# Buffers given out by products since their release, and another order of column pairs in the seventh stage

## The chip, the cores and the metric

The kernel runs on one core of a Trainium2 chip. The metric is the device time of one execution in microseconds (us), the median of the runs shown. One execution is also profiled; its span and its rows are what the profile below shows.

## The reference, cut to what matters

One step of a small decoder over 1024 prompt positions and 8 single sampled positions, with a model width of 2048. One layer pools and gates (mixer A), one attends in windows of 128 (mixer B); both end in an output projection and a layer norm. All in float32.

```python
def pool_layer(x, ...):                       # mixer A
    z = x @ w_in                              # 2048 -> 4096: u and gate
    d, new_state = multiscale_pool(u, prefix, pos)
    d = einsum('btgc,gce->btge', d, w_grp) * scale
    y = (d * silu(gate)) @ w_out              # 2048 -> 2048
    return layer_norm(ALPHA * x + y, g_ln, b_ln), new_state
...
k, v = shared_kv(h, pos, w_kv)
...
def attn_layer(x, ...):                       # mixer B
    z = x @ w_in                              # 2048 -> 4096: q and gate
    o = attn_core(q, kb, vb, ...)             # window of 128, with sinks
    y = (o * silu(gate)) @ w_out              # 2048 -> 2048
    return layer_norm(ALPHA * x + y, g_ln, b_ln)
```

## The kernel before

**Stages.** The positions are cut into two chunks, 0 (512 positions) and 1 (512 and the 8 sampled ones, 520 columns). The stages follow each other as `PHASES` lists them: `ai` of chunk 0 and 1 (input projection of mixer A), `ao` of 0 and 1 (its output projection), `bi` of 0 and 1 (keys, values, queries and gates of mixer B), `bo` of 0 and 1. `bo` of chunk 0, written `bo0`, is the seventh stage, and `bo1` the eighth and last.

**Products.** Nearly all matrix work is done as pairs of output columns (two blocks of 128 rows at a time), each by Strassen's and Winograd's scheme with seven products (`seven`, `pair`; the first two pairs of a locked stage run side by side in `both`). A product is 24 matmuls (lines 703 to 705): eight blocks of the contraction, and for each of them high part by high part, high by low, and low by high, because each float32 operand is split into a part rounded to float32r and the rest. `self.i` counts the products done; `end()` runs after each, and hands out the work that is due then.

**Weights.** A product needs one weight block of 128x1024 (512 KB). `load_to` loads it on SP's queue (line 292) some products ahead of its use (`self.ahead` is 7, 4, 3 for load, cast, rest in most stages), ACT casts it to its high part (line 517), and DVE subtracts for its low part (line 534). Four of the seven blocks of a pair are sums of the input's quarters; chunk 0 of `ai` and `bi` adds them on DVE and stores them to DRAM through POOL's queue (`swia`, `swib`; `swoa` and `swob` are made ahead by `sum_gen`), and later stages load them back. In `bo0` six low parts (`LOW`: blocks 5 and 6 of the pairs 5, 6 and 7) are stored as well, at line 536 (tensors `low55` to `low76`), and the last stage loads them instead of subtracting again.

**The moving operand.** At the start of a stage the seven combinations of its input are loaded (line 847, 14 loads of about 520 KB), cast (857) and subtracted (866). Four of the seven were computed before (`t_ops`, lines 914 to 918: tensors `tx`, `tg`, `th`, `to`), stored through POOL and loaded from DRAM.

**What sets the order.** PE, DVE and ACT execute in the order of the source (`in_order`). The instructions of SP and POOL are placed by the recording layer's scheduler, which can move a DMA behind others when the buffer that it fills comes free later. Each queue is executed in order: a load at the head of SP's queue that waits for its buffer holds all loads behind it.

**Buffers.** One pool, `Mem`, serves everything above: 54 buffers (tags m0 to m53), most of 1040 float32 a partition, which are also given out in halves. `release` notes for each half when it was released; `full` and `half` choose by that note. In the kernel before, the note is a count of releases (`self.clock`), with 10 added for a buffer that a DMA to DRAM still reads (`free(True)`, or `stored`), and the buffer with the lowest note is given out. `half` prefers a buffer with one half free if that half was released more than five releases ago, or if no more than three whole buffers are left. A buffer given out is not a buffer that is ready: whoever writes it first waits for its last user by semaphore.

**The output stage.** `phase_out` walks the pairs 0 to 7 in order: `x_in(p)` loads the residual (line 1347) one pair ahead, `done` adds it (1363), and `shifted` subtracts a common shift, stores the pair to `p0` (1408), squares it and adds it to the sums of the layer norm; the last pair frees the shift's buffer. `build_stream` lists the weight blocks in the same order.

Of the kernel before, what the change touches and what calls it, by code (L numbers as in the profile page):

```python
# [61 lines left out]
ORDERL = (0, 5, 2, 1, 3, 4, 6)  # L62
ENGINES = (mybir.EngineType.PE, mybir.EngineType.DVE, mybir.EngineType.Activation)
NSLOT, NWIDE = 54, 52
KEEP0 = 1

SPLIT = 4, 5, 6, 7
# [4 lines left out]

LATE = ()
LOW = TAIL[-6:]
FORM = (0, 1)
X_KEEP = 5
X_AGE = 3
# [23 lines left out]
class Slot:  # L101
# [40 lines left out]
class Mem:  # L142


    def __init__(self, pool, n):
        self.pool = pool
        self.t = [None] * n
        self.f = [[0, 0] for _ in range(n)]
        self.clock = self.n = 0

    def new(self, i):
        self.n += 1
# [3 lines left out]
    def whole(self):  # L156
        return [i for i, (a, b) in enumerate(self.f) if a is not None and b is not None]

    def full(self, n=2 * TMAX):
        i = min((i for i in self.whole() if i < NWIDE or n <= 1024), key=lambda i: max(self.f[i]))  # L160
        self.f[i] = [None, None]
        self.new(i)
        return Slot(self, i, None, self.t[i][:])

    def half(self, n=TMAX):
        fits = lambda i: i < NWIDE or n <= 512
        part = [
            (a if b is None else b, i) for i, (a, b) in enumerate(self.f) if (a is None) != (b is None) and fits(i)
        ]
        if part and min(part)[0] > self.clock - 6 and len(self.whole()) > 3:  # L170
            part = []
        i = min(part)[1] if part else min((i for i in self.whole() if fits(i)), key=lambda i: max(self.f[i]))
# [12 lines left out]


class Entry:
# [7 lines left out]
class Kern:  # L195
# [188 lines left out]
    def build_stream(self):  # L384
        io = self.io
        w = []
        for kind, c, part in PHASES:
            seven, locked = (kind, c, part) not in PLAIN, (kind, c) in LOCKED
            pr = (lambda name, q: self.next_pairs(name, [q], False)) if seven else self.plain_pair
            if seven and c == 0:  # L390
                pr = lambda name, q: (lambda f: [f[i] for i in ORDER7])(self.first_pair(name, q))
            if kind == "ai":
                for n in range(*part):
                    g, gates = divmod(n, 2)
                    for q in (8 * gates + 2 * g, 8 * gates + 2 * g + 1):
                        if n:
                            w += pr("wia", q)
                        elif c == 0:
                            e = self.bare_pair("wia", q)
                            w += [e[0], e[2], e[1], e[3]] if q == 0 else e  # L400
                        else:
                            f = self.first_pair("wia", q, False)
                            w += [f[i] for i in ORDER7]
                    for h in range(2 if gates else 0):
                        w.append(self.lone(io["wg"][g][:, h * 1024 : (h + 1) * 1024]))
            elif kind == "bi":
                if part[0] == 0:
                    w += self.next_pairs("wkv", range(2), locked) if seven else pr("wkv", 0) + pr("wkv", 1)
                if seven:
                    for p in range(*part):  # L410
                        for q in (p, 8 + p):
                            if c == 1 and p in FORM:
                                f = self.first_pair("wib", q, False)
                                w += [f[i] for i in ORDER7]
                            else:
                                w += pr("wib", q)
                else:
                    for p in range(*part):
                        q, g = ((self.bare_pair if p in FORM else pr)("wib", q) for q in (p, 8 + p))
                        w += q[:2] + g[:2] + q[2:] + g[2:]  # L420
            else:
                name = "woa" if kind == "ao" else "wob"
                if (kind, c, part) != PHASES[-1]:
                    prs = [self.next_pair(name, q) for q in range(8)]
                    if (kind, c) == ("bo", 0):
                        for q in LATE:
                            prs[q] = self.first_pair(name, q)
                        for q, i in LOW:
                            prs[q][i].keep = self.low[q, i]
                    w += [pr[i] for i in ORDERL for pr in prs[:2]]  # L430
# [132 lines left out]
    def end(self):  # L563
# [765 lines left out]
    def phase_out(self, c, res, nxt, last=None):  # L1329
# [11 lines left out]
        pre, xs = [], {}  # L1341
        whole = 8 if last is None else SPLIT[0]
# [6 lines left out]
        x_in(0)  # L1349
        box0 = []  # L1350
        pairs = []
        for p in range(whole):
            if p < 2:
                self.at(8 + 4 * p, lambda p=p: x_in(p + 1))
            else:
                self.at(6, lambda p=p: x_in(p + 1))
            if p == 6 and nxt is not None:
                self.x_begin(nxt)
            box, z0, z1 = self.two(T)

            def done(p=p, box=box):
                s, x = box["s"], xs.pop(p)
# [2 lines left out]
                )  # L1365
                x.free()
                if c == 0 or last is not None:
                    self.shifted(c, p, s, pre, acc, p == whole - 1)
                    return
                nc.gpsimd.dma_start(self.act["p", c][:, 2 * p : 2 * p + 2, :], self.pair_view(s, T))  # L1370
                if p == 0:
# [7 lines left out]
                    s.free(True)  # L1379

            pairs.append((z0, z1, done))
            self.last = p == 7
            if p == 1:
                self.both(c, *pairs)
            elif p > 1:
                self.pair(c, *pairs[p])
        self.last = False
        if last is not None:
            self.phase_end(c, xs, x_in, pre, acc(), *last)
# [3 lines left out]
    def shifted(self, c, p, s, pre, acc, end):  # L1393
# [20 lines left out]
        def add():  # L1414
# [1121 lines left out]
```

## Time and profile before

| | |
|---|---|
| median of 3 runs | 2298.36 us (2297.86 to 2299.89) |
| the profiled execution | 2298.91 us, of which its span 2297.1 us |
| PE busy with matmuls | 2277.5 us (99%) |
| DVE busy | 1903.4 us (83%) |
| ACT busy | 1387.8 us (60%) |
| POOL busy | 220.0 us (10%) |
| moved by DMA | 660.36 MB, 287 GB/s in the mean |

The span runs from the first instruction's start to the last one's end. A matmul of 260 columns stands with 283 ns in the profile, but the next one starts after about 0.12 us: matmuls overlap, so PE counts as busy even where it is only just fed, and the time it lost is read from the waits. DVE and ACT do not overlap with themselves in that way, so their busy time says how full they are.

### The profile page before, as it was taken

To read this page: it belongs to the slowest core of one execution; us is meant where nothing else is said; L and a number is where in the kernel's file an instruction comes from. 1 tells how busy PE (TensorE), PEld (TensorE's weight loads), DVE (VectorE), ACT (ScalarE), POOL (GpSimd) and SP (SyncE) were. 2 spreads that over 40 slices of the span, in tenths; PEclk is the share of its full clock that TensorE was granted. 3 is DMA by queue.
4 is the path that set the end of the run, shared out by engine and by line. 5 is a ranking of instruction groups with operands and counts; after the bars stand their busy time and mean duration, and the time that the engine had idled before them with its cause. 6 is when DMAs were issued, how large, how long until landed. Compare 5 with 4: busy or idle time off the path is not lost.

```text
span 2297.1 us, 50586 instructions
## 1 busy us (share of the span) xinstructions
PE 2277.5 (99%) x20333; PEld 2207.7 (96%) x20333; DVE 1903.4 (83%) x2429; ACT 1387.8 (60%) x2552; POOL 220.0 (10%) x405
## 2 busy tenths in 40 slices
PE   9999999999999999999999999999999999999998
PEld 8999999999999999999879999999999999999998
DVE  8888789877878898998878888899876777788897
ACT  5554446544546446655466667695766668756666
POOL 0111110011010010000111111101110110000001
PEclk9999999999999999999999999999999999999999
DMA  7779679988889999999677666787787878799896
GB/s 259 272 258 310 234 250 328 322 302 290 308 301 318 349 347 370 327 380 368 205 272 244 237 230 224 267 285 266 252 272 231 267 254 294 242 335 361 293 348 227
DMA packets 258684, 660.36 MB, mean 287 GB/s; under 512 B 28016, under 2 KB 117136, under 8 KB 258448
## 3 DMA queue, kind: packets, MB, share of 16 engines
q1 hardware_dynamic: 214432, 499.64, 64.0%
q0 software_dynamic: 44016, 157.48, 17.8%
q8 instruction: 159, 2.61, 0.5%
q14 instruction: 77, 0.63, 0.1%
HBM read 476.64 MB, written 180.38 MB: 286 GB/s over the span
## 4 chain that ended last, share of the span: by engine, by line
PE 51%; issue 4%; DMA 3%; DVE 2%; ACT 1%; SPq 0%; POOL 0%; DVEq 0%; POOLq 0%; ACTq 0%
PE pD L703 13%; PE pD L705 13%; PE pD L704 13%; PE pO L2003 2%; PE pD L731 2%; PE pD L733 2%; PE pD L732 2%; PE pS L1925 2%; PE pS L1978 1%; DMA m<-swob 1%; DMA m<-in_woa 1%; PE pS L2003 0%; DMA m<-in_wob 0%; DMA m<-swoa 0%; DVE m L534 0%
## 5 line engine op out<-in xcount | busy, mean ns | idle before, releaser
L703 PE MATMUL pD<-m,m 128*128 128x260 f32 (+1 forms) x5088 | 1440.9, 283 | 5.2 <-ACT pD L642 2.9
L705 PE MATMUL pD<-m,m 128*128 128x260 f32 (+1 forms) x5088 | 1433.2, 282 | 4.1 <-DVE m L534 4.1
L704 PE MATMUL pD<-m,m 128*128 128x260 f32 (+1 forms) x5088 | 1433.6, 282 | 0.0
L703 PEld LDWEIGHTS pD<-m,m 128*128 128x128 f32 x5088 | 957.9, 188 | 14.8 <-issue 7.2
L705 PEld LDWEIGHTS pD<-m,m 128*128 128x128 f32 x5088 | 958.8, 188 | 5.9 <-DVE m L534 5.9
L704 PEld LDWEIGHTS pD<-m,m 128*128 128x128 f32 x5088 | 958.1, 188 | 0.5
L534 DVE TENSOR_TENSOR m<-m,m 128x1024 fp32r<-128x1024 f32 x684 | 825.3, 1217 | 84.5 <-ACT m L517 36.9
L517 ACT CAST m<-m 128x1024 fp32r<-128x1024 f32 x690 | 720.2, 1049 | 243.1 <-DVE m L356 100.3
L356 DVE TENSOR_TENSOR m<-m,m 128x1024 f32<-128x1024 f32 x128 | 156.4, 1222 | 13.4 <-DMA m<-in_wia 7.8
L866 DVE TENSOR_TENSOR m<-m,m 128x1024 fp32r<-128x1024 f32 (+1 forms) x118 | 143.9, 1224 | 3.9 <-ACT m L857 3.1
L857 ACT CAST m<-m 128x1024 fp32r<-128x1024 f32 (+1 forms) x118 | 123.4, 1054 | 4.0 <-DMA m<-in_x 2.4
L664 DVE TENSOR_TENSOR m<-pD,m 128x260 f32<-128x260 f32 (+1 forms) x92 | 39.0, 424 | 103.3 <-ACT pD L663 94.7
L676 ACT COPY m<-pD 128x260 f32<-128x260 f32 (+1 forms) x88 | 32.8, 372 | 119.5 <-PE pD L705 119.0
L1961 ACT ACTIVATE m<-m,sm 128x128 f32<-128x128 f32 x256 | 99.3, 391 | 0.0
L1203 PE MATMUL pD<-m,m 128*128 128x260 f32 (+1 forms) x528 | 91.5, 323 | 0.0
L651 ACT COPY m<-pD 128x260 f32<-128x260 f32 (+1 forms) x92 | 34.4, 374 | 92.7 <-PE pD L705 92.5
L731 PE MATMUL pD<-m,m 128*128 128x512 f32 x224 | 89.0, 398 | 0.0
L733 PE MATMUL pD<-m,m 128*128 128x512 f32 x224 | 88.3, 394 | 0.0
L732 PE MATMUL pD<-m,m 128*128 128x512 f32 x224 | 88.1, 393 | 0.0
L1203 PEld LDWEIGHTS pD<-m,m 128*128 128x128 f32 x528 | 79.4, 188 | 8.2
L648 ACT COPY m<-pD 128x260 f32<-128x260 f32 (+1 forms) x90 | 33.6, 373 | 88.8 <-PE pD L705 87.2
L642 ACT ACTIVATE pD<-pD 128x260 f32<-128x260 f32 (+1 forms) x90 | 33.2, 369 | 82.2 <-PE pD L705 81.5
(262 smaller groups left out, 2140.1 us busy)
## 6 DMA issues: line engine op xcount, KB each, us to landing
m<-in_wib SPq DMA_DIRECT2D x132, 512.0 KB
m<-in_wia SPq DMA_DIRECT2D x128, 512.0 KB
m<-swoa SPq DMA_DIRECT2D x64, 512.0 KB
m<-swob SPq DMA_DIRECT2D x64, 512.0 KB
swia<-m POOLq DMA_DIRECT2D x56, 512.0 KB, 4.7
m<-swia SPq DMA_DIRECT2D x56, 512.0 KB
m<-in_woa SPq DMA_DIRECT2D x48, 512.0 KB
swib<-m POOLq DMA_DIRECT2D x48, 512.0 KB, 4.1
```

The lines of the kernel that those rows point to most:

```text
L356: self.nc.vector.tensor_add(s[out].a[:, :1024], s[x].a[:, :1024], s[y].a[:, :1024])
L517: self.nc.scalar.copy(hi.r[:, :1024], self.stream[self.cast].src().a[:, :1024])
L534: self.nc.vector.tensor_sub(lo.r[:, :1024], s.src().a[:, :1024], hi.a[:, :1024])
L703: nc.tensor.matmul(ps[:, :TH], wh[:, s], h, start=new and k == 0, stop=False, skip_group_check=on)
L704: nc.tensor.matmul(ps[:, :TH], wh[:, s], l, start=False, stop=False, skip_group_check=on)
L705: nc.tensor.matmul(ps[:, :TH], wl[:, s], h, start=False, stop=k == 7, skip_group_check=on)
L731: nc.tensor.matmul(ps[:], wh[:, s], h, start=par == 0 and k == 0, stop=False)
L732: nc.tensor.matmul(ps[:], wh[:, s], l, start=False, stop=False)
L733: nc.tensor.matmul(ps[:], wl[:, s], h, start=False, stop=par == 1 and k == 7)
L857: self.nc.scalar.copy(h.r[:, :n], s.a[:, :n])
L866: self.nc.vector.tensor_sub(l.r[:, :n], s.a[:, :n], h.a[:, :n])
L1203: nc.tensor.matmul(ps[:, : cs.stop - cs.start], ws[:, s], d[:, cs], start=f0 and k == 0, stop=l0 and k == 3,)
```

## The change

`Mem` now notes for each half of a buffer the product in which it becomes ready (`tick + late`, where `tick` is `self.i` and `late` is 1 for a buffer that was read last and 5 for one that is being stored) and the count of releases. `wait` turns that into the products still to go, never under 0, and the count. `full` and `half` take the buffer with the fewest products to go, and among equal ones the one released longest ago. A free half is passed over for a whole buffer if it is not ready yet and more than three whole buffers are left. Nothing waits for the numbers 1 and 5: they only rank the buffers.

The seventh stage takes its pairs in the order 0, 1, 4, 5, 6, 7, 2, 3, in `build_stream` (weights), in `phase_out` (residual loads, products, stores). The shift's buffer is freed after the last pair of that order.

```diff
 NSLOT, NWIDE = 54, 52
+READ, STORED = 1, 5
...
+PAIRS = 0, 1, 4, 5, 6, 7, 2, 3
...
     def free(self, stored=False):
-        self.mem.release(self, 10 if stored or self.stored else 0)
+        self.mem.release(self, STORED if stored or self.stored else READ)
...
+    def wait(self, *fs):
+        return max(max(0, ready - self.tick) for ready, _ in fs), max(clock for _, clock in fs)
+
     def full(self, n=2 * TMAX):
-        i = min((i for i in self.whole() if i < NWIDE or n <= 1024), key=lambda i: max(self.f[i]))
+        i = min((i for i in self.whole() if i < NWIDE or n <= 1024), key=lambda i: self.wait(*self.f[i]))
...
-            (a if b is None else b, i) for i, (a, b) in enumerate(self.f) if (a is None) != (b is None) and fits(i)
+            (self.wait(a if b is None else b), i)
+            for i, (a, b) in enumerate(self.f) if (a is None) != (b is None) and fits(i)
         ]
-        if part and min(part)[0] > self.clock - 6 and len(self.whole()) > 3:
+        if part and min(part)[0][0] and len(self.whole()) > 3:
             part = []
...
-            self.f[s.i][h] = self.clock + late
+            self.f[s.i][h] = self.tick + late, self.clock
...
-                    prs = [self.next_pair(name, q) for q in range(8)]
+                    prs = {q: self.next_pair(name, q) for q in (PAIRS if kind == "bo" else range(8))}
...
         self.i += 1
+        self.mem.tick = self.i
...
-        for p in range(whole):
-            if p < 2:
-                self.at(8 + 4 * p, lambda p=p: x_in(p + 1))
-            else:
-                self.at(6, lambda p=p: x_in(p + 1))
+        order = PAIRS if self.ph == "bo0" else range(whole)
+        for n, p in enumerate(order):
+            m = order[n + 1] if n + 1 < whole else whole
+            self.at(8 + 4 * n if n < 2 else 6, lambda m=m: x_in(m))
...
-                    self.shifted(c, p, s, pre, acc, p == whole - 1)
+                    self.shifted(c, p, s, pre, acc, c == 0 and p == order[-1])
...
-            if p == 7:
+            if end:
                 self.l_sh[c].free()
```

In the built program PE's order is the same row by row, save for the buffers and for which pair's blocks `bo0` takes. DVE's and ACT's order differ in two short places each. SP's and POOL's order differ in many. In the rows that follow, `m52_468_4074` is buffer m52, the 468th tile that the pool gave out; the last number only names the instruction's tile. Line numbers of the changed kernel are 8 to 10 higher.

POOL's queue in the seventh stage, before: the stores of the four `to1` combinations for the last stage, of the finished pairs (`p0`) and of the six low parts, the last of which stands right before the last pair's store.

```order
L918 DMA to1_93<-m37_2742_25839 128x1040
L1408 DMA p0_89<-m50_2738_25807 128x1024
L918 DMA to1_93<-m5_2753_25945 128x1040
L536 DMA low55_103<-m52_2755_25955 128x1024
L536 DMA low56_104<-m48_2766_26055 128x1024
L1408 DMA p0_89<-m6_2764_26051 128x1024
L536 DMA low65_105<-m10_2781_26192 128x1024
L536 DMA low66_106<-m52_2795_26298 128x1024
L1408 DMA p0_89<-m37_2793_26294 128x1024
L536 DMA low75_107<-m51_2812_26439 128x1024
L536 DMA low76_108<-m0_2832_26557 128x1024
L1408 DMA p0_89<-m27_2830_26553 128x1024
```

The same queue in the changed kernel:

```order
L545 DMA low55_103<-m33_2691_25453 128x1024
L545 DMA low56_104<-m45_2704_25557 128x1024
L928 DMA to1_93<-m9_2710_25620 128x1040
L1417 DMA p0_89<-m18_2702_25553 128x1024
L545 DMA low65_105<-m3_2719_25698 128x1024
L928 DMA to1_93<-m15_2723_25732 128x1040
L545 DMA low66_106<-m30_2732_25806 128x1024
L928 DMA to1_93<-m26_2734_25835 128x1040
L1417 DMA p0_89<-m9_2730_25802 128x1024
L928 DMA to1_93<-m3_2745_25941 128x1040
L545 DMA low75_107<-m28_2747_25951 128x1024
L545 DMA low76_108<-m6_2758_26051 128x1024
```

All six low stores moved ahead by two pairs (fourteen products); behind the last of them now stand three stores of pairs (`p0`), where one stood.

SP's queue at the change from `ai0` to `ai1`, before: weights of both stages, and the moving operand (`in_x1`, `tx1`) of the next.

```order
L847 DMA m40_432_3801<-in_x1 128x4x260
L292 DMA m14_418_3660<-in_wia 128x1024
L292 DMA m26_429_3769<-in_wia 128x1024
L847 DMA m41_433_3803<-in_x1 128x4x260
L292 DMA m22_434_3807<-in_wia 128x1024
L847 DMA m38_440_3848<-tx1_90 128x4x260
L292 DMA m3_443_3854<-in_wia 128x1024
L847 DMA m23_439_3846<-tx1_90 128x4x260
L292 DMA m21_442_3852<-in_wia 128x1024
L292 DMA m30_450_3921<-in_wia 128x1024
L292 DMA m14_460_4031<-in_wia 128x1024
L292 DMA m20_468_4074<-in_wg 128x1024
```

The same twelve loads in the changed kernel:

```order
L300 DMA m53_434_3807<-in_wia 128x1024
L300 DMA m52_418_3660<-in_wia 128x1024
L300 DMA m42_429_3769<-in_wia 128x1024
L857 DMA m23_432_3801<-in_x1 128x4x260
L857 DMA m11_433_3803<-in_x1 128x4x260
L300 DMA m15_443_3854<-in_wia 128x1024
L300 DMA m51_450_3921<-in_wia 128x1024
L857 DMA m41_439_3846<-tx1_90 128x4x260
L857 DMA m45_440_3848<-tx1_90 128x4x260
L300 DMA m44_442_3852<-in_wia 128x1024
L300 DMA m52_468_4074<-in_wg 128x1024
L300 DMA m2_460_4031<-in_wia 128x1024
```

Each goes into another buffer; the block of tile 434 moved ahead of four loads, that of 450 ahead of three, and that of 460 fell behind the group weights of 468.

More of the change, by code (lines that the diff above doesn't have):

```diff
@@ L147, in __init__ @@
         self.t = [None] * n
-        self.f = [[0, 0] for _ in range(n)]
-        self.clock = self.n = 0
+        self.f = [[(0, 0), (0, 0)] for _ in range(n)]
+        self.clock = self.n = self.tick = 0
     def new(self, i):
@@ L167, in half @@
         part = [
-            (a if b is None else b, i) for i, (a, b) in enumerate(self.f) if (a is None) != (b is None) and fits(i)
+            (self.wait(a if b is None else b), i)
+            for i, (a, b) in enumerate(self.f) if (a is None) != (b is None) and fits(i)
         ]
-        if part and min(part)[0] > self.clock - 6 and len(self.whole()) > 3:
+        if part and min(part)[0][0] and len(self.whole()) > 3:
             part = []
-        i = min(part)[1] if part else min((i for i in self.whole() if fits(i)), key=lambda i: max(self.f[i]))
+        i = min(part)[1] if part else min(
+            (i for i in self.whole() if fits(i)), key=lambda i: self.wait(*self.f[i])
+        )
         h = 0 if self.f[i][0] is not None else 1
@@ L1351, in phase_out @@
         pairs = []
-        for p in range(whole):
-            if p < 2:
-                self.at(8 + 4 * p, lambda p=p: x_in(p + 1))
-            else:
-                self.at(6, lambda p=p: x_in(p + 1))
-            if p == 6 and nxt is not None:
+        order = PAIRS if self.ph == "bo0" else range(whole)
+        for n, p in enumerate(order):
+            m = order[n + 1] if n + 1 < whole else whole
+            self.at(8 + 4 * n if n < 2 else 6, lambda m=m: x_in(m))
+            if n == 6 and nxt is not None:
                 self.x_begin(nxt)
@@ L1381, in phase_out @@
             pairs.append((z0, z1, done))
-            self.last = p == 7
-            if p == 1:
+            self.last = n == 7
+            if n == 1:
                 self.both(c, *pairs)
-            elif p > 1:
-                self.pair(c, *pairs[p])
+            elif n > 1:
+                self.pair(c, *pairs[n])
         self.last = False
```

1 line of the change is left out of this document (added).

## The prediction

> **What bounds the kernel now.** I read the page first, then the waits of TensorE, then the busy time in stretches, and last the entry of the last stage in the timeline.
>
> The page's span and its row of TensorE's clock, then the waits of TensorE's matmuls in the run (releaser, us in total, times, longest; two of 0.2 us left out):
>
> ```profile
> span 2297.1 us, 50586 instructions
> PEclk9999999999999999999999999999999999999999
> ```
>
> ```profile
> PE pD L705 <- DVE m L534: 4.1, 9, 0.9
> PE pD L703 <- ACT pD L642: 2.9, 3, 1.3
> PE pD L703 <- ACT m L657: 1.7, 2, 1.1
> PE pD L749 <- DVE m L2253: 1.3, 1, 1.3
> PE pD L703 <- ACT m L2188: 0.6, 1, 0.6
> PE pD L1630 <- POOL area L1656: 0.6, 1, 0.6
> PE pO L974 <- DVE m L958: 0.3, 1, 0.3
> ```
>
> They sum to 11.5 us, 0.5% of the span, and the clock was full in every slice. So TensorE sets the time, its own work isn't touched by the change, and 11.5 us less what the start and the end need is all that a better feeding can bring. What a worse feeding can cost has no such lid.
>
> Where the waits lie, from the busy time in stretches (stretch, its length, PE, PEld, DVE, ACT, POOL busy with counts, clock, DMA share, GB/s):
>
> ```profile
> 0.00:100.00 100.00, 96.51 (x577) 85.88 (x578) 83.58 (x102) 58.11 (x77) 6.37 (x19) 1.00 0.73 255
> 300.00:400.00 100.00, 98.08 (x778) 95.48 (x777) 95.25 (x108) 57.02 (x80) 7.91 (x17) 1.00 0.88 299
> 900.00:1000.00 100.00, 98.82 (x817) 97.95 (x816) 93.16 (x104) 62.49 (x87) 4.28 (x8) 1.00 0.97 350
> 2080.00:2100.00 20.00, 20.00 (x172) 20.00 (x171) 13.75 (x15) 12.23 (x18) 1.55 (x4) 1.00 0.96 365
> 2100.00:2120.00 20.00, 20.00 (x171) 20.00 (x170) 19.91 (x20) 14.31 (x18) 1.20 (x3) 1.00 1.04 366
> 2120.00:2140.00 20.00, 18.23 (x149) 17.79 (x148) 20.00 (x21) 15.87 (x23) 0.53 (x1) 1.00 1.03 383
> ```
>
> TensorE is idle 3.49 us in the first 100 us, 1.92 at the entry of the second stage, 1.18 at that of the fourth, and 1.77 between 2120 and 2140, at the entry of the last. DVE is full in all of these (95.25 and 93.16 of 100, 20.00 of 20), and the DMA engines in the last (1.04, 1.03). Between the entries there is next to nothing.
>
> **The change part by part.**
>
> *Order of pairs.* No instruction is added or removed. What moves at the end of the seventh stage is six stores of low parts, on POOL's queue. Two matmuls on one line, three apart, give the pace, and the POOL rows of the timeline the places (start, length, idle before):
>
> ```profile
> 2039.73 0.28 PE L703 MATMUL pD<-m,m 128*128 128x256 f32 x1
> ...
> 2040.08 0.28 PE L703 MATMUL pD<-m,m 128*128 128x256 f32 x1
> ```
>
> ```profile
> 2062.11 0.53 POOL L536 DMA_DIRECT2D low<-m  x1 [0.60 <-DVE m L534]
> ...
> 2080.47 0.53 POOL L536 DMA_DIRECT2D low<-m  x1 [0.37 <-DVE m L534]
> 2086.56 0.53 POOL L536 DMA_DIRECT2D low<-m  x1 [5.55 <-DVE m L534]
> ...
> 2101.38 0.53 POOL L536 DMA_DIRECT2D low<-m  x1 [1.24 <-DVE m L534]
> 2110.51 0.53 POOL L536 DMA_DIRECT2D low<-m  x1 [8.60 <-DVE m L534]
> ```
>
> A product is 24 matmuls of 0.117 us (0.35 / 3), 2.8 us; two pairs are fourteen products, 39 us. So the stores at 2101.38 and 2110.51 go to about 2062 and 2071, and the first from 2062.11 to about 2023. The `p` stores keep their places, since each position still ends one pair.
>
> What stood in the way there, by the waits between 2090 and 2135, the ACT rows of the timeline, and the row of the chain that ended last:
>
> ```profile
> ACT m L517 <- DMA m<-swob: 4.1, 4, 2.7
> PE pD L703 <- ACT m L657: 1.1, 1, 1.1
> PE pD L703 <- ACT pD L642: 0.6, 1, 0.6
> ```
>
> ```profile
> 2129.07 1.06 ACT L517 CAST m<-m 128x1024 fp32r<-128x1024 f32 x1 [2.67 <-DMA m<-swob]
> ...
> 2130.98 0.37 ACT L657 COPY m<-pD 128x260 f32<-128x260 f32 x1
> ```
>
> ```profile
> 2117.81 11.18 DMA m<-swob
> ```
>
> A weight block took 11.18 us from its issue at 2117.81; ACT stood 2.67 us for it, the copy of line 657 is queued behind that cast, and TensorE waits 1.1 us for the copy. The 0.6 us ahead of it has the same form. All of it is DMA bandwidth: a stretch with a share of 1.03 moves 383 GB/s. A low store is 524,288 bytes, 1.4 us at (366 + 383) / 2 GB/s. Two of them out of this stretch make its later loads land 2.8 us sooner, which is more than the 2.67 us that ACT stood.
>
> The Trainium skill ("DMA: Bandwidth & Descriptors", section on the anatomy of one DMA) fits a transfer as about 2.0 us fixed and its bytes at 436 GB/s, by which the two would free 2.4 us, a little under 2.67; the trace's full stretches stay at 366 and 383, so I keep the larger figure.
>
> What is late next is DVE. Its first idle time after the crowd:
>
> ```profile
> 2143.21 0.43 DVE L664 TENSOR_TENSOR m<-pD,m 128x260 f32<-128x260 f32 x1 [1.30 <-PE pD L705]
> ```
>
> At 2143.21 it had waited 1.30 us for TensorE, so a TensorE that comes 1.77 us sooner finds DVE 0.47 us behind here. The term lies between 1.30 and 1.77 if the loads are what counts, and is 0 if DVE's queue inside the crowd, which has no idle time at all, is already what feeds TensorE. I take -1.5; ends -1.8 and 0.
>
> Where the stores go, the cost is that of two low stores in a stretch like 2080 to 2100: it holds two (at 2080.47 and 2086.56), with a share of 0.96, and TensorE lost 0.00 there. I take 0; ends 0 and +1.1 (the wait above, if it comes up there). The buffers of the low parts are also back 39 us sooner at the crowded end, which I count in the same term. Of the stores of pairs, 2 and 3 change places with 6 and 7: pairs 2 and 3 are now stored last, as 6 and 7 were, and are wanted only in the last stage's layer norm: 0.
>
> *The rule for buffers.* It changes which buffer a load or a cast gets, so whom it waits for, and with that SP's order. The waits of SP's queue (same columns), and the landing times of the low stores:
>
> ```profile
> SPq L292 <- PE pD L705: 342.7, 152, 8.9
> SPq L292 <- DVE m L534: 182.8, 88, 9.2
> SPq L292 <- DMA to<-m: 43.6, 9, 8.7
> SPq L292 <- DMA swoa<-m: 29.9, 7, 8.5
> ```
>
> ```profile
> DMA to landing us min/median/max: 5.4/7.7/8.6
> ```
>
> A load waits mostly for the last reader of its buffer, 2.3 us in the mean (342.7 / 152), and in a few cases 8.5 us for a store. Ten releases are, by the tile numbers in SP's order (34 tiles, 434 to 468, over five weight loads, about 7 a product), one and a half products, 4 us: shorter than a store's 5.4 to 8.6. Five products are 14 us, which covers it. So the waits for stores (73.5 us in the two rows) should fall, and loads will more often take a buffer that was only read. But nothing behind SP is idle for it in mid-stage: weights are issued seven products ahead and cast four ahead, which leaves three products, 8.5 us, and TensorE doesn't wait there. Only at the entries, where the pool is short and DVE full, does a load's time pass on. For the second stage's entry (waits from 340 to 420):
>
> ```profile
> PE pD L705 <- DVE m L534: 1.9, 3, 0.9
> PE pD L703 <- ACT pD L642: 1.3, 1, 1.3
> DVE m L356 <- DMA m<-in_wia: 1.3, 1, 1.3
> ```
>
> DVE lost 1.3 us there on one load, and is full else; SP's new order moves blocks both forward and back in the same place. Ends: -1.3 (that load comes in time) and +4.6 (two more waits of the mean length, in a crowd where nothing hides them). I take 0, since the moves go both ways. The few moved rows on DVE and ACT lie in stages where TensorE doesn't wait: 0.
>
> Sum: -1.5 + 0 + 0 + 0, from the profiled execution's 2298.91 to 2297.4. The median of the runs stands 0.55 below that execution: 2296.9.
>
> **The rivals.**
>
> *DVE hides it.* DVE's 19.91 and 20.00 of 20 speak for it: if its subtractions feed TensorE just in time, earlier loads change nothing, and the buffers' rule cancels out. Against it: the two waits there end on ACT rows behind a DMA, none on DVE's line 534. Time: unchanged, 2298.4.
>
> *The rule helps at every entry.* Of the 11.5 us, 3.5 are in the first 100 us, where the pool has hardly been round once, and 0.6 at the end (line 1630). If four fifths of the other 7.4 go, 5.9: 2292.5. For it: SP's waits for stores. Against it: at the second and fourth entries the longest part is DVE's own queue.
>
> *A load gets a buffer that is still read* (slower). A buffer read in the last product counts as ready in the next one, although its reader may stand far back on a full DVE (a wait for line 534 of up to 9.2 us is in the rows). Such a load at SP's head holds all behind it. In mid-stage the 8.5 us cover it; at an entry, where a load alone took 11.18 us, they don't, and each further us passes through ACT and DVE to TensorE. It decides as soon as two such heads fall into the entries of stages 2, 4 or 8: two mean waits are 4.6 us, with one long one among them 2.3 + 8.9 less the 1.5 won and some slack, about 6: 2304. For it: block 460 fell back in SP's order at the second entry. Against it: the old rule had the same blindness.
>
> The Trainium skill ("TensorE: Matmul & The Clock Gate", Part 1) has an idle stretch of about 3.4 us halve TensorE's clock for the next window; by that a wait of the long kind would cost some 1.7 us more. The longest wait here is 1.3 us and the clock row is full, so no run here shows it.
>
> **How the numbers follow.** Forecast (between 2295.5 and 2297.9): 0.43. DVE hides it (2298.4, give or take 1): 0.22. Every entry (2290.5 to 2293.8): 0.21. Slower (2303 and more): 0.14. A difference under 0.2%, 4.6 us, is what runs of this kernel can't tell from none: faster 0.23 (the third case and a little of the first), same 0.63, slower 0.14. The range from 2291.5 to 2303 leaves out the far part of the two outer cases, under 0.2.
>
> **What would show it.** The low stores of line 536 some 39 us earlier; in the crowd of the last entry ACT's wait for `swob` under 1 us, and TensorE busy over 19.5 of 20 where it was 18.23. SP's waits for `to`, `swoa` and `g` smaller, those for line 705 larger. The second and fourth entries within 1 us of before. I am wrong if the crowd keeps its 1.77 us with the stores gone (then DVE feeds it), or if new waits on line 534 or 642 stand at an entry.

## The result and the profile after

The changed kernel takes 2302.73 us, the median of 15 runs (2298.73 to 2308.2), beside 2298.86 us of before (15 runs, 2296.62 to 2301.21): a ratio of 1.0017, 95% interval 1.001 to 1.0024, slower by some 3.9 us. The forecast was 2296.9. The profiled execution took 2303.87 us, 1.1 above its median.

The page of the changed kernel, its span and clock row, and then the waits of TensorE's matmuls (line waiting, releaser, us in total, times, longest; eight smaller rows left out):

```profile
span 2302.1 us, 50582 instructions
...
PEclk9999999999999999999999999999999999999999
```

```profile
PE pD L715 <- DVE m L543: 4.9, 10, 0.9
PE pD L713 <- ACT pD L652: 2.3, 2, 1.3
PE pD L713 <- ACT pD L673: 2.2, 1, 2.2
PE pD L759 <- DVE m L2262: 1.3, 1, 1.3
PE pD L713 <- ACT m L667: 1.2, 1, 1.2
PE pD L713 <- ACT m L2197: 0.7, 1, 0.7
...
```

One wait is of a kind that before did not have: 2.2 us, once, for the copy of line 673. Stretches of the changed kernel (columns as in the prediction), and last the third one's counterpart in the kernel before:

```profile
900.00:1000.00 100.00, 99.35 (x824) 98.69 (x824) 93.62 (x101) 64.67 (x90) 4.27 (x8) 1.00 0.97 354
...
2120.00:2140.00 20.00, 20.00 (x167) 19.81 (x166) 20.00 (x20) 14.39 (x20) 0.53 (x1) 1.00 1.05 390
880.00:900.00 20.00, 17.77 (x148) 17.46 (x148) 15.45 (x18) 10.30 (x15) 1.27 (x2) 1.00 1.04 395
```

```profile
880.00:900.00 20.00, 20.00 (x172) 20.00 (x171) 17.64 (x20) 14.05 (x19) 1.27 (x2) 1.00 0.99 332
```

TensorE has the 20.00 of 20 at the last stage's entry that the order of pairs was to bring (also from 2127 to 2147, where the work of before's 2120 to 2140 now lies), and loses 2.23 between 880 and 900, at the entry of the fourth stage, where before lost nothing.

The two traces have the same 20333 matmuls in the same order, so the start of the k-th in one less that in the other says where time is lost. In us, at points of before's time, for the kernels that matter below:

```
                  340   880   900  1100  1260  1590  1660  1930  1970  2110  2150  2230  2270
changed kernel   -0.1  +0.2  +3.0  +1.7  +2.2  +2.5  +5.7  +5.7  +7.0  +7.1  +5.1  +4.9  +4.9
rule_only        -0.3  -0.5  +3.1  +1.5  +4.8  +5.1  +5.8  +5.9  +5.9  +5.6  +6.5  +6.4  +6.4
pairs_only       -0.0  -0.0  -0.0  -0.6  -0.6  -0.6  -0.6  -0.1  +1.5  +1.7  -0.2  +2.8  +2.8
pairs_p20        +0.1  -0.2  -0.2  +0.3  +0.3  +0.3  +0.3  +0.3  -0.0  +0.1  -1.8  -1.8  -1.9
wob9             -0.5  -1.0  -0.8  -1.8  -1.0  -1.2  +1.4  +1.5  +2.1  +2.1  +0.2  +0.1  +0.0
stored8          -0.3  -0.2  +6.8  +8.7  +9.7 +10.7 +10.7 +14.0 +16.6 +16.5 +14.6 +15.5 +15.5
to_loads6        -0.3  -0.7  -0.6  -1.3  -1.6  -1.7  +4.9  +6.7  +6.6  +6.6  +5.7  +5.6  +5.6
loads_shy1_ao    -1.0  -0.6  -0.4  -2.2  -1.4  -1.4  -1.3  -0.8  -1.4  -1.2  -2.4  -2.5  -2.5
```

The changed kernel loses 2.8 us at one place near 889, 3.2 between 1590 and 1660 in steps of at most 1.3, and 1.3 near 1950, and wins 1.3 between 900 and 1100 and 2.0 at 2124 to 2131. The rest is small.

Small entries of this table may be chance. Up to about 1960 `pairs_only` and `pairs_p20` are the program of before, instruction by instruction. Still the first loses 1.6 us between 1930 and 1970 and the second does not, and between 900 and 1100 they move by 0.6 and 0.5 us in opposite directions.

**The place near 889.** SP's waits in the changed kernel from 862 to 876, then rows of SP's, ACT's and TensorE's timelines (start, length, idle before):

```profile
SPq L857 <- DMA swob<-m: 6.9, 1, 6.9
SPq L300 <- DMA swob<-m: 3.0, 1, 3.0
```

```profile
865.52 0.38 SPq L1357 DMA_DIRECT2D m<-in_x  x1
872.89 1.48 SPq L857 DMA_DIRECT2D m<-g  x3
...
875.77 0.59 SPq L300 DMA_DIRECT2D m<-in_woa  x1
```

```profile
887.12 1.04 ACT L526 CAST m<-m 128x1024 fp32r<-128x1024 f32 x1 [5.18 <-DMA m<-in_woa]
888.07 1.05 ACT L867 CAST m<-m 128x1040 fp32r<-128x1040 f32 x1
889.03 0.36 ACT L673 COPY pD<-pD 128x256 f32<-128x256 f32 x1
```

```profile
889.45 0.39 PE L713 MATMUL pD<-m,m 128*128 128x256 f32 x1 [2.23 <-ACT pD L673]
```

A load of `g` has been given a buffer out of which a block of `swob` is still being stored. SP stands 6.9 us for the landing, between 865.52 and 872.89, and everything behind that load stands with it. The block of in_woa that ACT wants next goes out at 875.77, in a burst with the other loads that were held, and has landed only by 887.12, 11.3 us later; ACT stands 5.18 us for it, and the copy of line 673, which TensorE needs, is queued behind that cast on ACT. Before, SP's longest wait for a store in this stretch is 0.9 us, the same block goes out 5.6 us sooner, and the copy (line 663 there) starts 3.5 us sooner:

```profile
SPq L847 <- DMA p<-m: 0.9, 1, 0.9
```

```profile
870.15 0.81 SPq L292 DMA_DIRECT2D m<-in_woa  x1
```

```profile
885.56 0.37 ACT L663 COPY pD<-pD 128x256 f32<-128x256 f32 x1
```

**What the rule did to SP.** The view of SP's waits, changed kernel:

```profile
SPq L300 <- PE pD L715: 320.6, 144, 8.9
SPq L300 <- DVE m L543: 144.2, 76, 7.4
SPq L466 <- DMA swoa<-m: 94.1, 19, 9.0
...
SPq L300 <- DMA swoa<-m: 49.5, 10, 8.9
...
SPq L300 <- DMA to<-m: 20.1, 3, 9.9
```

All its rows add to 1683 us, before's to 1689: SP stands as long as ever, but for something else. The waits for stores (`rows` left out) went from 307 us in 77 to 407 in 97, those for `swoa` alone from 45 to 144 (before had 29.9 us on line 292 and this row):

```profile
SPq L457 <- DMA swoa<-m: 15.0, 4, 5.4
```

In the two programs one can count who takes a buffer that had been stored last. Of 354 such, loads on SP's queue took 116 before and 152 after, casts and subtractions most of the rest; in the products that run from about 350 to 910 us it was 22 of 73 and 50 of 76. Yet these buffers were on average older: 4.8 products since their release, 4.3 before.

Two lines of the code explain it, as I read them; the runs on who takes the stored buffers, further down, test it. Under the new rule a stored buffer comes of age on a product's edge, and `begin` calls `load_to` first, before `prep_to` and `cast_to`: a load is the first to see it. Under the old one a buffer's rank rises release by release, so it may come up anywhere in a product. A cast or a subtraction that takes such a buffer comes late in its own engine's queue and seldom waits: in before ACT and DVE together stood 8.3 us for stores, in eight waits, the longest 2.1. A load waits at the head of SP's queue.

### The profile page after: what moved, and what is told of

The parts are those of the page before. It is cut to its first block, busy times and chain, and to the rows that moved or that the text cites. A ratio compares the mean times of both kernels' runs of the same rounds, so it can differ in the third digit from the quotient of the medians.

```text
span 2302.1 us, 50582 instructions
## 1 busy us (share of the span) xinstructions
PE 2278.9 (99%) x20333; PEld 2207.5 (96%) x20333; DVE 1905.4 (83%) x2429; ACT 1386.4 (60%) x2552; POOL 220.0 (10%) x405
## 4 chain that ended last, share of the span: by engine, by line
PE 86%; DVE 6%; DMA 3%; issue 1%; ACT 1%; SPq 0%; DVEq 0%; POOL 0%; ACTq 0%; POOLq 0%
PE pD L713 24%; PE pD L715 23%; PE pD L714 23%; PE pD L1213 3%; PE pO L2012 2%; PE pD L741 2%; PE pD L743 2%; PE pD L742 2%; DVE m L543 2%; PE pS L1934 1%; PE pS L1987 1%; DVE m L364 1%; DVE m L876 1%; DMA m<-rows 0%; DMA m<-in_wia 0%
## 5 line engine op out<-in xcount | busy, mean ns | idle before, releaser
L686 ACT COPY m<-pD 128x260 f32<-128x260 f32 (+1 forms) x88 | 32.7, 372 | 113.7 <-PE pD L715 112.6
L1970 ACT ACTIVATE m<-m,sm 128x128 f32<-128x128 f32 x256 | 99.2, 390 | 0.0
L661 ACT COPY m<-pD 128x260 f32<-128x260 f32 (+1 forms) x92 | 34.4, 374 | 90.5 <-PE pD L715 90.5
L1983 ACT ACTIVATE m<-m,sm 128x128 f32<-128x128 f32 x256 | 81.9, 393 | 4.3 <-DVE sm L1978 4.1
```

## The experiments

Each was timed in five rounds beside the kernel before on the same chip; ratios are to before, with 95% intervals.

**The parts alone.** `pairs_only`: the kernel before with the new order and all that hangs on it, and the old rule.

```diff
+PAIRS = 0, 1, 4, 5, 6, 7, 2, 3
...
+        order = PAIRS if self.ph == "bo0" else range(whole)
```

> The kernel before with the order of pairs 0, 1, 4, 5, 6, 7, 2, 3 in the seventh stage, and the old rule for buffers. Theory A (the two parts act apart: the order wins what was forecast for it, the rule loses more): TensorE's waits of 1.77 us at the entry of the last stage go, nothing else moves, about 2 us under before: 2296 to 2298. Theory B (the order itself is the loss, for instance because pairs 2 and 3 are stored last): 2300 to 2303, as in the changed kernel.

2300.95 us, ratio 1.0007 (0.9998 to 1.0016): theory B's range, 3 us above theory A's, though 1 is still inside the interval. The 1.9 us at 2124 to 2131 came as theory A has it, and two losses stand beside it: 1.6 us between 1930 and 1970, which is chance of this execution, since the program is still that of before there, and 3.1 between 2200 and 2230. The second one in its rows (SP's waits 2180 to 2200, all engines' waits to 2217):

```profile
SPq L297 <- DMA p<-m: 9.6, 1, 9.6
```

```profile
DVE m L1463 <- DMA m<-h: 3.3, 1, 3.3
...
PE pD L711 <- DVE m L540: 2.6, 2, 1.5
```

The same form as near 889, under the old rule: a load of swob stands 9.6 us for a store to `p`, a load of `h` behind it reaches DVE 3.3 us late, and TensorE waits 2.6 us for DVE. Whether the order must cost this, or a buffer's chance does, is left to `pairs_p20`.

`rule_only`: the changed kernel with the old order.

```diff
-PAIRS = 0, 1, 4, 5, 6, 7, 2, 3
+PAIRS = 0, 1, 2, 3, 4, 5, 6, 7
```

> The changed kernel with the pairs in the order 0 to 7 again; the new rule for buffers stays. Theory A: the rule alone costs 6 to 7 us (2.4 at the entry of the fourth stage, some 2.7 between 1594 and 1651, 1 at the entry of the seventh stage), so 2304 to 2306, and TensorE waits 2.2 us near 889 as in the changed kernel. Theory B (the order is the loss): 2298 to 2300.

2305.48 us, ratio 1.0027 (1.0017 to 1.0037): theory A. The rule is the loss, and TensorE again waits near 889, 1.85 us.

**The two numbers of the rule.** `stored8` has eight products for a stored buffer, `stored4` four; `read2` has two for one that was read.

```diff
-READ, STORED = 1, 5
+READ, STORED = 1, 8
```

> The changed kernel with eight products for a stored buffer instead of five. Theory A1 (five products are too short for a store that stands in POOL's queue behind DVE; SP then waits for its landing and holds every load behind it): SP's waits for stores, 407 us in 97 in the changed kernel, fall under half, the wait near 889 goes, and the time falls by 3 to 6 us to 2297 to 2300. Theory A2 (the loss is read buffers handed out while still read): younger read buffers, 1.75 products old instead of 2.04, so SP's waits for readers grow and the time is the same or more, 2302 to 2307.

2314.93 us, ratio 1.0069 (1.0056 to 1.0081): both theories fail. SP's waits for stores fell only to 332 us, and the wait near 889 grew to 4.9 us. Waiting longer does not keep loads off stored buffers: they still took 128 of 353, and SP stood 7.1 us for swob between 860 and 896.

> The changed kernel with four products for a stored buffer instead of five. With eight the time rose by 12 us, because the buffers that were only read are then given out younger (1.75 products old in the mean instead of 2.04). If that balance is what counts, four give 2299 to 2301.5, with fewer waits for readers at the entries; if stores are what SP must be kept from, four give 2304 to 2308.

2305.89 us, ratio 1.0038 (1.0025 to 1.0052): the second reading, with 450 us of waits for stores and a wait of 3.2 us near 889. So of four, five and eight the five is best (six and seven were not run), and neither of the others mends the place.

> The changed kernel with two products for a buffer that was only read instead of one; a stored one keeps five. Stored buffers are then taken a little younger (4.5 products in the mean instead of 4.8). Theory A1 (stores): SP's waits for stores stay or grow, and the time stays at 2302 to 2305. Theory A2 (readers): SP's waits for readers fall and with them TensorE's waits; 2297 to 2300.

2301.13 us, ratio 1.0012 (1.0003 to 1.0021): between the two ranges. Against A1 the time fell 1.6 us below the changed kernel's; against A2 SP's waits for readers did not fall (1107 us in the changed kernel, 1115 here). SP stands 6.4 us for swob here too, but some 10 us later: the block of in_woa that came too late in the changed kernel had gone out at 869.83, ahead of that wait, and TensorE does not wait near 889. Where the wait stands decides, not its length.

**The rule by stages.** `old_mid` deals by the old rule in the second to fourth stages, `new_mid` in the other five.

```diff
+OLD = ("ai1", "ao0", "ao1")
...
+        if self.old:
+            return max(key for _, _, key in fs), 0
...
+        self.mem.old = getattr(self, "ph", "ai0") in OLD
```

> The changed kernel with the old rule for buffers in the second, third and fourth stages (about 350 to 1090 us) and the new one elsewhere; the new order of pairs stays. Theory C (the new rule's loss is SP standing for a store in these stages, above all 7 us near 870 for a store of swob, behind which the loads of the fourth stage's entry come late): SP's waits for stores between 350 and 910, 205 us in the changed kernel and 81 before, fall to about 80, the wait of 2.2 us near 889 goes, and the time falls by 2 to 3 us: 2299.5 to 2301. Theory D (any new deal of buffers puts some load of an entry behind a long wait, wherever the rule changes): the wait near 889 goes, but others of 1 to 3 us come, and the time stays between 2301.5 and 2304.

2300.85 us, ratio 1.0005 (0.9996 to 1.0013): theory C in its range, SP's waits for stores from 350 to 910 at 69 us and no wait near 889. TensorE lost some 1.8 us near 1594, where the changed kernel loses too, and 1.9 between 1100 and 1260, so part of theory D holds: other losses of its size came.

> The reverse: the old rule for buffers everywhere but in the second, third and fourth stages, which have the new one; new order of pairs. Theory C: the loss near 889 stands (2.0 to 2.4 us), and little else: 2301.5 to 2304. Theory D: no foretelling of where, 2299 to 2304; the place near 889 may be clean, since the deal at the start of the second stage differs.

2305.59 us, ratio 1.0026 (1.0016 to 1.0036): the wait near 889 is there (1.88 us), but the time is 1.6 above the range of theory C and of theory D; the profile has another wait of 1.8 us at 1962.

**One store alone.** `wob9` changes only how long the buffers of one kind of sum count as busy in one stage.

```diff
-            s.free(True)
+            self.mem.release(s, 9 if self.ph == "ao0" else STORED)
```

> The changed kernel with one thing more: in the third stage alone, a buffer of the sums of wob (stored to swob) is given out nine products after its release instead of five. Theory C: SP no longer stands 7 us near 870 for that store, the loads behind it are 5 to 7 us earlier, ACT's wait of 5.2 us for in_woa and TensorE's 2.2 us near 889 go, 2299.5 to 2301. Theory D: another wait takes its place at the same entry, 2302 to 2305.

2298.96 us, ratio 0.9997 (0.9989 to 1.0006): 3.8 us less than the changed kernel. The largest row of SP's waits from 860 to 880:

```profile
SPq L857 <- DVE m L543: 3.0, 2, 2.3
```

No wait for swob is left there, ACT's row for in_woa is gone, and the table shows +0.2 us between 880 and 900 where the changed kernel shows +2.8. This is the cause of the largest single loss, shown by its removal; it makes up 2.6 of the 3.8 us. SP's waits for stores in the whole program are still 401 us, so most of their growth costs nothing. The time is 0.5 us under theory C's range.

**Who takes the stored buffers.** `loads_shy1` is the changed kernel in which a load ranks a stored buffer one product younger than a cast does:

```diff
+    def wait(self, *fs, load=False):
+        late = 1 if load else 0
...
+            max(max(0, ready + late * stored - self.tick) for ready, _, stored in fs),
...
-            s[k] = self.mem.full(1024)
+            s[k] = self.mem.full(1024, True)
```

`to_loads6` is the kernel before, in which casts and subtractions rank it six releases younger; `old_shy6` is the old rule and the new order, with the same mark at the loads instead:

```diff
+        late = lambda i: 6 if away and any(self.late[i]) else 0
...
-            hi = self.mem.full(1024)
+            hi = self.mem.full(1024, True)
```

> The changed kernel, in which a load counts a stored buffer as one product younger than a cast or a subtraction does. In the tables of the two kernels, of the buffers that had been stored, loads on SP's queue took 116 of 354 before and 152 of 354 in the changed kernel, and 50 of 76 instead of 22 of 73 between 350 and 910 us, where SP's waits for stores grew from 81 to 205 us; here they take 25. Theory E (the rule's loss comes from that: five products end on a product's edge, where the loads choose first, and SP then stands for the landing with all its other loads behind it): SP's waits for stores fall from 407 us to under 120, the wait of 2.2 us near 889 goes, and the time is 2297 to 2300. Theory F (SP's waits are only renamed, a load now waits as long for a reader on PE or DVE): the sum of SP's waits stays near 1683 us, and the time stays at 2301 to 2305.

2298.96 us, ratio 0.9999 (0.999 to 1.0008): theory E's time, with 53 us of waits for stores left and no wait near 889. Theory F's sum holds as well: SP's waits add to 1694 us, now for readers:

```profile
SPq L304 <- PE pD L719: 537.9, 203, 9.0
SPq L304 <- DVE m L547: 207.9, 110, 6.5
```

Both are true: the sum is renamed, and the new name costs less.

> The reverse: the kernel before (old rule, old order), in which casts and subtractions count a stored buffer as six releases younger, so that loads take 182 of them instead of 116. Theory E: SP's waits for stores rise from 307 to 400 us and more, TensorE gets new waits at the entries, above all at the fourth stage's, and the time rises by 2 to 6 us to 2301 to 2305, though the rule is the old one. Theory F: 2297.5 to 2300.

2305.62 us, ratio 1.0028 (1.0018 to 1.0038): theory E, 0.6 us above its range, and the strongest run for it, since rule and order are those of before and only the taker differs. Waits for stores are 462 us. The place was foretold wrong: nothing near 889, but 6.6 us between 1590 and 1660 (4.33 of them a wait of TensorE, most of the rest a halved clock behind it; see the last section). Rows of DVE and TensorE there, and SP's longest wait of 1570 to 1590:

```profile
1594.60 0.43 DVE L1789 TENSOR_TENSOR m<-m,m 128x260 f32<-128x260 f32 x1 [9.35 <-DMA m<-rows]
```

```profile
1597.15 0.58 PE L707 MATMUL pD<-m,m 128*128 128x260 f32 x1 [4.33 <-DVE m L536]
```

```profile
SPq L459 <- DMA swob<-m: 5.6, 1, 5.6
```

A load of in_wob stands 5.6 us for a store of swob; behind it stands the load that brings `rows` back, for which DVE waits in order. Before has no such wait in its row of this kind; the changed kernel has one of 5.26 us at the same place (before's row first):

```profile
1586.88 0.42 DVE L1787 TENSOR_TENSOR m<-m,m 128x260 f32<-128x260 f32 x1
```

```profile
1594.65 0.43 DVE L1796 TENSOR_TENSOR m<-m,m 128x260 f32<-128x260 f32 x1 [5.26 <-DMA m<-rows]
```

> The old rule with the new order of pairs, in which a load counts a stored buffer as six releases younger; loads take 11 stored buffers instead of 116. Theory E: SP's waits for stores fall from 307 to under 100 us, the entries lose what they wait for stores (the 2.6 us at 2211 to 2217 with the order alone), and the time is 2295 to 2298.5. Theory F: 2299 to 2303, as with the order alone.

2301.91 us, ratio 1.0009 (1.0 to 1.0018): theory F's range, and theory E's missed, though only 36 us of waits for stores were left. TensorE waited 2.11 us at 352, at the second stage's entry, for a load that now stood for readers.

**The second stage apart.** `old_shy6_ao` and `loads_shy1_ao` are shy from the third stage on only.

```diff
-        late = 1 if load else 0
+        late = 1 if load and self.on else 0
...
+            self.mem.on = kind != "ai"
```

> The old rule with the new order of pairs, in which a load counts a stored buffer as six releases younger, but only from the third stage on; the first two stages deal as before. Theory G (keeping loads from stored buffers is right, and the loss of the run with it in all stages was the second stage's entry, where TensorE waited 2.1 and 1.3 us for line 534 near 352 and 407 behind a load of in_wia that came 2.8 us late): these waits go back to those of before, and the time is 2296 to 2298.5. Theory H (that rule costs elsewhere, and keeping SP from stores buys nothing once loads wait for readers): 2299 to 2302.

2297.95 us, ratio 0.9999 (0.999 to 1.0008): theory G. The wait at the second stage's entry is back at 1.27 us. By the medians this kernel takes 4.0 us less than `old_shy6`, but not all of that is the second stage's: the two traces part by 2.4 us there, and by 1.8 near 1950, where chance is as large.

> The changed kernel, in which a load counts a stored buffer as one product younger, but only from the third stage on. The second stage then has the new rule's own deal, with SP standing for swoa 22 times. Theory G: the entry of the second stage is that of the changed kernel (TensorE waits less than 1.5 us near 352), that of the fourth stays clean, 2297 to 2299. Theory H: 2299.5 to 2302.

2297.0 us, ratio 0.9994 (0.9986 to 1.0003): theory G, 5.7 us under the changed kernel.

**The order again.** `pairs_p20` is `pairs_only` with one store ranked younger.

```diff
             if p >= KEEP0:
-                s.free(True)
+                self.mem.release(s, 20 if self.ph == "bo1" else 10)
```

> The new order of pairs under the old rule, with one thing more: in the last stage a buffer stored to p counts as twenty releases younger instead of ten. In the run with the order alone a load of swob stood 9.6 us for a store to p, a load of h behind it came 3.3 us late for DVE, and TensorE waited 2.6 us at 2211 to 2217. Theory A (order and rule act apart, and that wait is a buffer's chance in the last stage): that wait goes, 2296.5 to 2299.5. Theory B (the order itself costs, elsewhere): 2300 to 2302.

2297.6 us, ratio 0.9993 (0.9984 to 1.0002): theory A. The wait for `p` is gone and so are the 3 us at 2200 to 2230; the table shows one gain, 1.9 us at 2124 to 2131. So the loss of `pairs_only` in the last stage was a matter of one buffer, and not of the order.

No version is measurably faster than before; `loads_shy1_ao` and `pairs_p20` are 5.7 and 5.1 us under the changed kernel's median, and 1 to 2 us under before's, with 1 still inside their intervals.

## Why the prediction was wrong, point by point

- *Order of pairs, -1.5 (ends -1.8 and 0).* Right in place and sign, a little small. The six low stores went where they were said to: the changed kernel's first and last, in a trace that runs 7 us late there,

```profile
2027.98 0.54 POOL L545 DMA_DIRECT2D low<-m  x1 [0.37 <-DVE m L543]
...
2074.84 0.53 POOL L545 DMA_DIRECT2D low<-m  x1 [5.14 <-DVE m L543]
```

  and TensorE's 1.77 us at 2120 to 2140 went. With the rule left out and the wait for `p` mended, the order is worth 1.8 us in the profile (span 2295.3 beside 2297.1), 1.3 by the medians. All thirteen kernels with the new order gain 1.2 to 2.0 us between 2110 and 2150; of the two others with the old one `rule_only` loses 0.9 and `to_loads6` gains 0.9. One sign failed: ACT's wait for `swob` in the crowd, to fall under 1 us, is 4.0 us in the changed kernel (four waits, longest 2.3), 3.9 in `loads_shy1_ao` and 1.8 in `pairs_p20` (two, longest 1.02). So the gain is shown, and the way that the prediction gives it, through ACT's wait, only in part. "DVE hides it" fell.
- *Where the stores go, 0.* Held: where they now run, in the stretches from 2020 to 2080, the changed kernel's TensorE is busy 20.00 of 20 with a DMA share of 0.96 to 1.02. But the order alone also let a store to `p` meet a load in the last stage, which no step had looked for.
- *The rule, 0 (ends -1.3 and +4.6).* This is the step that failed. `rule_only` puts it at +6.5 us (2305.48 beside 2298.94); that is above the upper end, though the interval, 3.9 to 8.5, reaches below it. SP's waits for stores, which "should fall", rose from 307 to 407 us; the prediction had taken them from two rows, 73.5 us, a quarter of what all rows hold. Three sentences of it were wrong. "Five products are 14 us, which covers it" compared a landing with an age: the buffers were indeed older, and SP waited more for them, because it runs ahead until some buffer stops it and loads took more of these. Loads did not "more often take a buffer that was only read"; they took 36 stored ones more. And the cover of "8.5 us" in mid-stage holds for weights issued seven products ahead, not for the loads that stand between them: DVE stood 5.26 us for `rows` at 1594. SP's signs came out mixed: `to` and `g` smaller (20.1 and 16.6 us), `swoa` larger (94.1 and 49.5), line 715 smaller (320.6), where it was to grow. The fourth entry, to stay within 1 us, lost 2.8; the second stayed.
- *"The moves go both ways".* They did, 1.2 us was won near 925 and 1020, part of which may be chance, but they do not cancel: an earlier load wins nothing where TensorE doesn't wait, a later one costs once its slack is used up.
- *The rivals.* The third one (0.14) named the end, 2304, and the mechanism, a load at SP's head with a buffer still in use, and the entry of the fourth stage. It had the holder wrong: it looked for a reader on DVE, and it was a store. Its sum, one long wait and one mean one, is not what happened either, so that 2304 lies close to 2302.73 is luck. "The rule helps at every entry" fell.
- *What bounds the kernel.* One reading was off, and nothing was added up from it: DVE is not full in the first 100 us, with 83.58 of 100.

What stays open: why the changed kernel's `rows` came late at 1594. SP's waits there are 4.2 us for `to` ahead of it and 4.1 for `rows` itself, and no run took them apart. The 1.3 us near 1950 are no more than the chance that `pairs_only` shows there, and `stored8` loses 6 us more after 1590 that were not traced.

## What to carry to other kernels

With one in-order queue for loads, ask of every rule that hands out buffers who will take the one with the long release: a load that gets it stops all loads behind it, a compute result that gets it waited little here. The sum of such a queue's waits says little (1682 to 1718 us in all sixteen profiles, from 2297 to 2315 us); look at what stands behind the longest single waits and when it is due. And a buffer that is ready by the clock of the plan isn't ready by the clock of a queue that runs ahead of the plan.

## What the runs showed of the hardware that was not expected

A short idle of TensorE costs more than its length. After the 4.9 us near 889 in `stored8` the granted clock stays at half for some 4 us (stretches of that run; the clock is the number behind POOL's):

```profile
885.00:891.50 6.50, 1.75 (x15) 1.55 (x14) 3.83 (x5) 2.17 (x3) 0.72 (x1) 0.82 1.05 393
891.50:894.00 2.50, 2.34 (x11) 2.34 (x12) 1.89 (x3) 0.83 (x2) 0.00 (x0) 0.50 1.03 413
894.00:897.00 3.00, 3.00 (x20) 3.00 (x20) 1.23 (x1) 1.66 (x3) 0.00 (x0) 0.68 0.24 90
897.00:900.00 3.00, 3.00 (x28) 3.00 (x27) 2.85 (x3) 0.41 (x2) 0.00 (x0) 1.00 0.81 247
```

The table has +6.8 us at 900 for it, where -0.2 stood at 880: some 2 us more than the idle time. In kind that agrees with the Trainium skill ("TensorE: Matmul & The Clock Gate", Part 1), by which an idle window of about 3.4 us halves the clock for the next. But here the clock fell some 2.4 us into the wait, before a whole window had been idle (a mean of 0.82 over 885 to 891.5 is half a clock for its last 2.4 us), and much shorter idle times did it too. In `rule_only` after 1.85 us, in `old_shy6` after 2.11 (the clock is 0.60 and 0.51):

```profile
888.30:890.50 2.20, 2.17 (x11) 2.17 (x12) 2.19 (x4) 1.55 (x2) 0.00 (x0) 0.60 1.02 417
```

```profile
354.00:356.00 2.00, 2.00 (x11) 2.00 (x11) 2.00 (x3) 1.69 (x3) 0.00 (x0) 0.51 0.97 352
```

Over all profiles, of ten idle times from 1.8 to 4.9 us eight were followed by matmuls of 415 ns where 283 is usual, and none of the 27 from 1.1 to 1.5 us (the program's start left out). The changed kernel's own 2.23 us was one of the two that were not.

What decides is how the idle time falls on a grid. In each of the sixteen traces all changes of the clock lie a whole number of steps of 3.413 us apart, and the first change comes between 4.4 and 7.4 us, at another time in each execution. Of the steps that ran at full clock nine held 1.60 to 2.37 us of idle time, and the step after each of them ran at half; none of the others, with 1.57 us or less, was followed by half a clock. The two nearest to the line are a step of the changed kernel, and one of `stored4` with the step behind it:

```profile
885.38:888.79 3.41, 1.84 (x16) 1.63 (x14) 3.25 (x5) 1.67 (x2) 0.72 (x1) 1.00 1.04 381
```

```profile
1250.43:1253.84 3.41, 1.81 (x13) 1.43 (x12) 3.34 (x6) 2.28 (x11) 0.00 (x0) 1.00 1.03 413
1253.84:1257.26 3.42, 3.42 (x19) 3.42 (x18) 2.93 (x5) 3.42 (x11) 0.00 (x0) 0.50 0.38 115
```

The grid cuts the changed kernel's 2.23 us into 1.57 and 0.66, and nothing follows; `stored4` has two waits of 1.03 and 0.56 us in one step, and the clock is halved. So in these traces somewhat under half a step of idle time was enough. By these figures a wait of 1.6 to 3.2 us may or may not be followed by half a clock, as the execution has it, and a longer one always is; that is an estimate from sixteen traces.

One half step costs some 1.5 us on top (24 matmuls in a mean step of 186 ns instead of 122), and the three waits over 3 us cost 1.9 to 2.5. `rule_only`'s profile has two half steps, so its distance to the changed kernel is not the order's gain alone, and the prediction's price for such a case, 1.7 us for a wait of the long kind, was right in size and too strict in its condition.
